# A selection step queued behind the last one-hot compare in a two-layer decoder step with product-key experts

## The chip, the cores and the metric

One core of one Trainium2 chip runs the whole program. The metric is the time of one execution on the device, in microseconds (us). The engines are TensorE (PE; PEld is its weight load), VectorE (DVE), ScalarE (ACT), GpSimd (POOL) and SyncE (SP), which issues most loads. An engine works through its own queue in order.

## What is computed

Two layers of a decoder trunk on 512 prompt tokens and 64 sample tokens, model width 1024, all in fp32. Each layer has token mixers (windowed attention, gated linear attention, pooling) and then a PEER channel mixer, which is where the change lies:

```python
def block(xi):                                   # 128 tokens
    q = jnp.einsum('td,dhk->thk', xi, w_query).reshape(128, 8, 2, 128)
    s = jnp.einsum('thpk,hpnk->thpn', q, sub_keys)
    sv, si = lax.top_k(s, 16)                    # top 16 of 128 keys, both halves
    cand = sv[:, :, 0, :, None] + sv[:, :, 1, None, :]
    cidx = si[:, :, 0, :, None] * 128 + si[:, :, 1, None, :]
    cscore, ci = lax.top_k(cand.reshape(128, 8, 256), 16)
    eidx = jnp.take_along_axis(cidx.reshape(128, 8, 256), ci, axis=-1)
    g = jax.nn.softmax(cscore, axis=-1)
    u = jnp.take(u_tab, eidx, axis=0)
    h = jax.nn.gelu(jnp.einsum('thkd,td->thk', u, xi), approximate=False)
    v = jnp.take(v_tab, eidx, axis=0)
    return jnp.einsum('thk,thkd->td', g * h, v)
```

So each token selects, for each of 8 heads, 16 of 16384 single-neuron experts, and sums their gated outputs.

## The kernel before

The tokens are split. For tokens 0 to 383 the channel mixer is computed densely: the 16384 experts are 128 blocks of 128, every block is computed for all 384 tokens (`expert_h`, then the matmuls into `y`), and the gates, zero where an expert was not selected, are laid out as a dense table in DRAM (`gd`). For tokens 384 to 511 and the 64 sample tokens the selected rows are gathered by indirect DMA (class `Gather`) beside the dense loop. Matmuls of the dense part are made from fp32 split into two parts of fp32r (`hi`, `lo`; three products); the first 12 experts use whole fp32 weights.

Python code traces the instructions; a planner then gives every engine its order, from what is ready in its own model of the machine and from a rank, which is the place in the trace. `tc.high_priority(n)` moves the rank ahead by n instructions (a negative n, back). `tc.issue_after(ins)` makes what is traced in its block on the engine of `ins` come behind `ins` in that engine's queue; it adds no wait for the end of `ins`.

Per layer, in the order of the trace around the change (function `tile_hybrid_step`):

- Line 1174, `_query`: scores and top 16 of the tokens 256 to 511, two tiles of 128 tokens. `sv` and `siu` hold the values and indices; they, the whole copy `x1W` of the tokens, and all work tiles of the selections lie in the pool `sel` (`sp`, line 1163).
- Line 1188, `_slots`: selection (`_select`, some 150 VectorE instructions and one Exp on ScalarE) of tokens 256 to 383 and its transposition on TensorE into `sT2`.
- Line 1190: the matmuls and Gelu of the first LA = 12 experts (`expert_h`) on `x1W`. `h` has LA + 2 = 14 buffers, its PSUM tile `ps_h` two.
- Lines 1191 to 1194, `_spread`: 32 one-hot steps of 4 tokens, in the pool `spread`. Each compares token keys with an iota on VectorE (lines 951, 953, 960), scales by the gate (953's part on ScalarE, line 958), multiplies one-hots on TensorE (line 964) and copies the result into `gst` (ScalarE, line 965). After 8 steps `gst`, one buffer, is stored to `gd` by four DMAs of ScalarE's queue (line 971). `oh` has two buffers, `ps_yr` six. Rank 250 ahead (SPREAD).
- Lines 1195 to 1197, `gat.choose`: selection of tokens 384 to 511 (`_select`, then lines 996 and 997), which gives the row numbers `gidx` and the gates `gB` of the gather. Rank 50 back (LAGS). It issues no DMA here (line 1000 is for the sample tokens).
- Line 1198 closes the pool `sel`. Line 1208 opens the pool `dense` in the room that the two closed pools leave; its tiles are `vr`, `vh`, `vl`, `wh`, `wl`, `gt`.
- Lines 1210 to 1239: the dense loop over 128 experts. `n.tick()` puts the gathers of the samples, then of tokens 384 to 511, between the experts.

Of the kernel before, what the change touches and what calls it, by code (L numbers as in the profile page):

```python
# [16 lines left out]
OP = mybir.AluOpType  # L17
# [27 lines left out]
LAGS = -50  # L45
# [895 lines left out]
def _spread(n, gp, t, sT, new_ps, gt0=None):  # L941

    nc, c = n.nc, n.c
    iota = lambda w: c["iota"][:, None, None, :].to_broadcast([128, w, 4, 128])
    for g in range(128 // GT):
        st = gp.tile([128, 128, GT], F32, name="gst", bufs=n.gst)
        for t4 in range(0, GT, 4):
            tt = g * GT + t4
            oh = gp.tile([128, 2, 4, 128], F32, name="oh", bufs=n.job)
            w = n.act_mul  # L950
            nc.vector.tensor_tensor(oh[:, 1], iota(1)[:, 0], sT[:, 1, tt:tt + 4, None].to_broadcast([128, 4, 128]), op=OP.is_equal)  # L951
            if w:
                nc.vector.tensor_tensor(oh[:, 0, 0:w], iota(1)[:, 0, 0:w], sT[:, 0, tt:tt + w, None].to_broadcast([128, w, 128]),  # L953
                                        op=OP.is_equal)
            for k in range(4):
                gate = sT[:, 2, tt + k:tt + k + 1]
                if k < w:
                    nc.scalar.activation(oh[:, 0, k, :], oh[:, 0, k, :], AF.Copy, scale=gate)
                else:
                    nc.vector.tensor_scalar(oh[:, 0, k, :], c["iota"], sT[:, 0, tt + k:tt + k + 1], gate,  # L960
                                            op0=OP.is_equal, op1=OP.mult)
            ps = new_ps().rearrange("p (a b) -> p a b", a=4)
            for k in range(4):
                nc.tensor.matmul(ps[:, k, :], oh[:, 1, k, :], oh[:, 0, k, :], start=True, stop=True)  # L964
            nc.scalar.copy(st[:, :, t4:t4 + 4], ps.rearrange("p t i -> p i t"))
            if t4 + 4 < GT:
                yield
        if gt0 is not None:
            nc.scalar.copy(gt0[:, t * (128 // GT) + g], st[:, 0:4, :])
        for i in range(4):  # L970
            nc.scalar.dma_start(n.gd[t * (128 // GT) + g, :, i * 32:(i + 1) * 32, :], st[:, i * 32:(i + 1) * 32, :])
        yield
# [72 lines left out]
def tile_hybrid_step(ctx, tc, I, O, L):  # L1045
    nc = tc.nc
    n = Net(ctx, tc, I, O, L)
# [57 lines left out]
    for l in range(L):  # L1105
# [18 lines left out]
        sT = [sa.tile([128, 3, 128], F32, name=f"selT{t}") for t in range(2)]  # L1124

        def first():
            yield from gat.choose(n, l, sa, sv, siu, 2, 1)
            gs = gat.slots(1)
            for t in range(2):
                for k, _ in enumerate(itertools.chain(_slots(n, sa, sv, siu, t, sT[t], n.hring),  # L1130
                                                      _spread(n, sa, t, sT[t], n.hring))):
                    if k % 2 == 0 and n.early:
                        n.early -= 1
                        next(gs)
                    yield
            n.gs = gs
# [28 lines left out]
        for q in range(2):  # L1165
            nc.gpsimd.tensor_tensor(x1W[q][:, :, 0:HB], x1A[0][q][:, :, 0:HB].bitcast(F32), x1A[1][q][:, :, 0:HB].bitcast(F32),
                                    op=OP.add)
# [23 lines left out]
        with tc.tile_pool(name=f"spread{l}", bufs=1) as gp:  # L1191
            with tc.high_priority(SPREAD):
                for _ in _spread(n, gp, 2, sT2, new_y, gt0):
                    pass
        with tc.high_priority(LAGS):
            for _ in gat.choose(n, l, sp, sv, siu, 1, 0):
                pass
        sc.close()
# [231 lines left out]
```

## Time and profile before

| | us |
|---|---|
| median of 3 runs | 4738.8 (4728.3 to 4741.7) |
| the profiled execution, its own time | 4737.0 |
| its span in the trace | 4735.2 |
| TensorE busy | 4530.7 (96% of the span) |
| VectorE busy | 3793.4 (80%) |
| ScalarE busy | 1820.2 (38%) |
| GpSimd busy | 1370.1 (29%) |

Busy time is an average over stages with different limits, so a change in one stage is read from that stage: from the busy time in a stretch of the span, and from the timeline of each engine there. In a timeline a row is a start, a duration, engine, line, operation, output<-input, count, and in brackets how long the engine had been idle before it and what ended that. Rows of several instructions are merged. The two layers show the same stages, at 1237 to 1369 and at 3592 to 3724 us for the part around the change.

### The profile page before, as it was taken

How to read it: one execution, taken by the hardware profiler on the slowest of the kernel's cores; microseconds unless marked ns; L12 is line 12 of the kernel's file. 1: busy time of each engine (PE TensorE's matmuls, PEld its weight loads, DVE VectorE, ACT ScalarE, POOL GpSimd, SP SyncE). 2: the span in 40 equal slices, each digit the busy share in tenths (PEclk: the TensorE clock that was granted, in tenths of full speed). 3: DMA queues.
4: the chain of work that ended last, by engine and by line, in shares of the span. 5: the costliest groups of instructions: out<-in, count | busy, mean ns of one | idle time of the engine just before them, and what ended most of it. 6: DMA issues, size and time to landing. Idle time of an engine off the chain costs nothing. (4 is left out here: it accounts for less than half of the span.)

```text
span 4735.2 us, 69451 instructions
## 1 busy us (share of the span) xinstructions
PE 4530.7 (96%) x25588; PEld 4001.3 (85%) x25588; DVE 3793.4 (80%) x7435; ACT 1820.2 (38%) x3386; POOL 1370.1 (29%) x884
## 2 busy tenths in 40 slices
PE   7999999989999999999999999999999999999998
PEld 6879977788778999999878789777887789999997
DVE  5455698697879999999964556977978799999998
ACT  3434323354343433333344343234433433333333
POOL 0011001121035555555300110011210365555552
PEclk9999999999999999999999999999999999999999
DMA  4334535566379899999723345265663798898996
GB/s 147 110 125 139 180 94 213 193 232 229 126 274 345 328 337 325 330 324 331 279 85 121 122 149 167 88 222 195 232 231 131 289 353 323 328 330 322 335 323 233
DMA packets 359521, 1093.59 MB, mean 231 GB/s; under 512 B 28495, under 2 KB 164175, under 8 KB 309709
## 3 DMA queue, kind: packets, MB, share of 16 engines
q1 hardware_dynamic: 272112, 608.88, 38.0%
q0 software_dynamic: 55296, 402.68, 22.6%
q10 hardware_dynamic: 31772, 77.60, 4.4%
q8 instruction: 201, 3.29, 0.3%
q14 instruction: 140, 1.14, 0.1%
HBM read 1014.01 MB, written 77.52 MB: 231 GB/s over the span
## 5 line engine op out<-in xcount | busy, mean ns | idle before, releaser
L128 POOL TENSOR_TENSOR wlo<-raw,whi 128x1024 fp32r<-128x1024 f32 x232 | 704.1, 3035 | 928.4 <-ACT whi L131 894.1
L131 ACT CAST whi<-raw 128x1024 fp32r<-128x1024 f32 x582 | 607.9, 1048 | 601.0 <-PE ps_mm L183 379.0
L183 PE MATMUL ps_h<-x1A,whi 128*128 128x384 f32 x3712 | 696.4, 340 | 13.3 <-ACT h L1182 13.2
L183 PEld LDWEIGHTS ps_h<-x1A,whi 128*128 128x128 f32 x3712 | 655.9, 190 | 33.6 <-ACT h L1182 17.1
L128 DVE TENSOR_TENSOR wlo<-raw,whi 128x1024 fp32r<-128x1024 f32 x350 | 432.8, 1241 | 275.2 <-ACT whi L131 136.8
L1024 DVE SCALAR_TENSOR_TENSOR zB<-uvr,hc,zB 128x1024 f32<-128x1024 f32 x380 | 587.2, 1545 | 4.7
L1006 POOL DMA_INDIRECT uvr<-uv,gidx x384 | 441.8, 1151 | 474.9 <-DVE zB L1024 209.0
L1017 DVE SCALAR_TENSOR_TENSOR uvr<-uvr,x1B 128x1024 f32<-128x1024 f32 x384 | 493.4, 1285 | 68.9 <-DMA uvr<-uv,gidx 68.6
L1236 PE MATMUL y<-vh,wh 128*128 128x512 f32 x1536 | 478.1, 393 | 0.6 <-ACT vh L131 0.6
L1236 PE MATMUL y<-vl,wh 128*128 128x512 f32 x1536 | 476.5, 391 | 0.0
L1236 PE MATMUL y<-vh,wl 128*128 128x512 f32 x1536 | 474.9, 390 | 0.3 <-DVE wl L128 0.3
L183 PE MATMUL ps_mm<-xa,whi 128*128 128x320 f32 x2400 | 413.3, 321 | 14.7 <-ACT xa L131 14.7
L1225 DVE TENSOR_TENSOR h<-h,gt 128x384 f32<-128x384 f32 x256 | 395.8, 1551 | 11.5 <-ACT h L1182 7.0
L183 PEld LDWEIGHTS ps_mm<-xa,whi 128*128 128x128 f32 x2400 | 370.7, 194 | 33.8 <-ACT xa L131 15.3
L183 PE MATMUL ps_h<-x1A,wlo 128*128 128x384 f32 x1856 | 362.7, 338 | 0.0
L1236 PEld LDWEIGHTS y<-vl,wh 128*128 128x128 f32 x1536 | 288.7, 188 | 64.2 <-DVE vl L128 0.2
L1236 PEld LDWEIGHTS y<-vh,wl 128*128 128x128 f32 x1536 | 288.7, 188 | 63.5 <-DVE wl L128 0.7
L131 ACT CAST wh<-h 128x384 fp32r<-128x384 f32 x256 | 130.5, 511 | 533.3 <-PE y L1236 502.0
L183 PEld LDWEIGHTS ps_h<-x1A,wlo 128*128 128x128 f32 x1856 | 327.1, 189 | 0.0
L1236 PEld LDWEIGHTS y<-vh,wh 128*128 128x128 f32 x1536 | 287.3, 189 | 45.7 <-ACT vh L131 1.4
L1019 ACT ACTIVATE hc<-hc 128x1 f32<-128x1 f32 x384 | 77.7, 203 | 628.1 <-DVE uvr L1017 620.3
L128 DVE TENSOR_TENSOR vl<-vr,vh 128x1024 fp32r<-128x1024 f32 x256 | 311.5, 1217 | 0.7 <-ACT vh L131 0.7
(349 smaller groups left out, 7650.3 us busy)
## 6 DMA issues: line engine op xcount, KB each, us to landing
raw<-wall SPq DMA_DIRECT2D x468, 512.0 KB
raw<-ut SPq DMA_DIRECT2D x256, 512.0 KB
vr<-vt SPq DMA_DIRECT2D x256, 512.0 KB
gd<-gst ACTq DMA_DIRECT2D x96, 512.0 KB
gt<-gd SPq DMA_DIRECT2D x62, 768.0 KB
S<-state_gla SPq DMA_DIRECT2D x8, 1024.0 KB
s_gla<-S ACTq DMA_DIRECT2D x8, 1024.0 KB
uvr<-uv,gidx POOLq DMA_INDIRECT x384
```

What stands on the lines that cost most here:

```text
L128: return eng.tensor_tensor(lo, src, hi.bitcast(F32), op=OP.subtract)
L131: return self.nc.scalar.copy(hi, src), self.sub_lo(lo, src, hi, eng)
L183: self.nc.tensor.matmul(ps[:, 0:W], w[wi][:, k * 128:(k + 1) * 128], xs[xi][k], start=(a == 0 and k == 0), stop=(a == len(pa) - 1 and k == ...
L1006: self.n.nc.gpsimd.indirect_dma_start(out=r, out_offset=None, in_=self.n.I["uv"], in_offset=bass.IndirectOffsetOnAxis(ap=self.idx[t][:, s: ...
L1017: nc.vector.scalar_tensor_tensor(r[:, 0:1024], r[:, 0:1024], 1.0, self.x[t], op0=OP.mult, op1=OP.mult, accum_out=hc[:, 0:1])
L1019: nc.scalar.activation(hc[:, 1:2], hc[:, 0:1], AF.Gelu)
L1024: nc.vector.scalar_tensor_tensor(acc, r[:, 1024:2048], hc[:, 1:2], acc, op0=OP.mult, op1=OP.add)
L1225: nc.vector.tensor_tensor(h3, h3, gt[:, :, i % 4, :], op=OP.mult)
L1236: nc.tensor.matmul(y[t][d], wt[:, ts], vt[:, d * 512:(d + 1) * 512], start=(j == 0 and a == 0), stop=(j == NE - 1 and a == 2))
```

## The change

The last compare of line 951 that was traced is kept in `n.spread`, and the instructions that `gat.choose` traces on VectorE for tokens 384 to 511 are queued behind it. At that place the last one traced is the compare of the 32nd step of `_spread` for tokens 256 to 383.

```diff
@@ _spread
-            nc.vector.tensor_tensor(oh[:, 1], iota(1)[:, 0], sT[:, 1, tt:tt + 4, None].to_broadcast([128, 4, 128]), op=OP.is_equal)
+            n.spread = nc.vector.tensor_tensor(oh[:, 1], iota(1)[:, 0], sT[:, 1, tt:tt + 4, None].to_broadcast([128, 4, 128]), op=OP.is_equal)
@@ tile_hybrid_step
-        with tc.high_priority(LAGS):
+        with tc.high_priority(LAGS), tc.issue_after(n.spread.ins):
             for _ in gat.choose(n, l, sp, sv, siu, 1, 0):
                 pass
```

## Rows read from the trace of the kernel before

**Rows 1.** The page: busy us (share of the span) and instructions of each engine.

```profile
PE 4530.7 (96%) x25588; PEld 4001.3 (85%) x25588; DVE 3793.4 (80%) x7435; ACT 1820.2 (38%) x3386; POOL 1370.1 (29%) x884
```

**Rows 2.** Windows: length, busy PE, PEld, DVE, ACT, POOL, PE clock, DMA share, GB/s.

```profile
1236.90:1263.40 26.50, 24.29 (x72) 14.02 (x73) 25.83 (x159) 5.32 (x8) 0.00 (x0) 0.94 0.20 63
1263.40:1325.50 62.10, 61.31 (x301) 43.38 (x300) 49.36 (x150) 35.65 (x82) 4.71 (x3) 1.00 0.43 151
1325.50:1365.70 40.20, 29.93 (x179) 28.76 (x177) 25.57 (x42) 19.05 (x43) 13.92 (x6) 0.88 0.54 200
1380.00:2360.00 980.00, 977.30 (x4911) 884.73 (x4910) 920.47 (x1057) 378.13 (x642) 519.16 (x272) 1.00 0.90 328
```

**Rows 3.** Timeline of TensorE around the start of the dense stage, first layer.

```profile
1359.31 1.79 PE L183 MATMUL ps_h<-x1A,wlo 128*128 128x384 f32 x8
1365.74 2.93 PE L183 MATMUL ps_h<-x1A,whi 128*128 128x384 f32 x8 [4.65 <-ACT h L1182]
```

**Rows 4.** Timelines of ScalarE and SyncE there; the last row is the second layer's.

```profile
1356.72 2.89 ACTq L971 DMA_DIRECT2D gd<-gst  x4
...
1363.97 0.92 ACT L131 CAST wh<-h 128x384 fp32r<-128x384 f32 x2 [2.93 <-DMA gd<-gst]
...
1364.08 0.80 SPq L1219 DMA_DIRECT2D vr<-vt  x2
...
3718.97 0.81 SPq L1219 DMA_DIRECT2D vr<-vt  x2
```

**Rows 5.** Timeline of VectorE: selection's first and last, last compares; last row second layer.

```profile
1247.32 0.28 DVE L887 TENSOR_TENSOR cand<-sv 128x128 f32<-128x128 f32 x1
...
1306.86 0.29 DVE L997 TENSOR_TENSOR gidx<-key 128x128 int32<-128x128 f32 x1
...
1354.20 0.59 DVE L960 TENSOR_SCALAR oh<-ct,selT 128x128 f32<-128x128 f32 x2
1357.05 1.97 DVE L1225 TENSOR_TENSOR h<-h,gt 128x384 f32<-128x384 f32 x4 [2.25 <-ACT gt L969]
...
3709.84 0.59 DVE L960 TENSOR_SCALAR oh<-ct,selT 128x128 f32<-128x128 f32 x2
```

**Rows 6.** Windows, VectorE alone (DVE busy first); the last row: one-hot tiles, every engine.

```profile
1263.40:1308.70 45.30, 43.26 (x134) 1.00 0.45 161
1239.06:1308.70 69.64, 66.93 (x278) 0.98 0.37 128
...
1239.06:1308.70 69.64, 20.04 (x146) 18.99 (x147) 28.75 (x76) 12.86 (x38) 0.98 0.37 128
```

**Rows 7.** Windows of the one-hot tiles: busy PE, PEld, DVE, ACT, with counts.

```profile
1263.40:1325.50 62.10, 24.59 (x176) 23.50 (x176) 34.86 (x92) 15.63 (x46) 1.00 0.43 151
```

**Rows 8.** Timeline of VectorE: the compare of line 906 in both selections, and what followed.

```profile
1248.21 1.22 DVE L906 TENSOR_TENSOR rstep<-ci,rank 128x2048 bf16<-128x2048 bf16 x1
1249.34 0.19 DVE L887 TENSOR_TENSOR cand<-sv 128x40 f32<-128x40 f32 x1
...
1283.39 1.23 DVE L906 TENSOR_TENSOR rstep<-ci,rank 128x2048 bf16<-128x2048 bf16 x1
1284.65 1.22 DVE L861 TENSOR_TENSOR rprod<-rstep,di 128x2048 bf16<-128x2048 bf16 x1
```

**Rows 9.** Timelines of VectorE and POOL: one-hot compares without and beside POOL's split.

```profile
1347.18 0.42 DVE L953 TENSOR_TENSOR oh<-ct,selT 128x256 f32<-128x256 f32 x1
...
1351.70 2.58 DVE L953 TENSOR_TENSOR oh<-ct,selT 128x256 f32<-128x256 f32 x1
...
1351.48 2.52 POOL L128 TENSOR_TENSOR wlo<-raw,whi 128x1024 fp32r<-128x1024 f32 x1 [8.57 <-PE ps_h L183]
1361.23 2.34 POOL L128 TENSOR_TENSOR wlo<-raw,whi 128x1024 fp32r<-128x1024 f32 x1 [7.23 <-ACT whi L131]
```

**Rows 10.** Windows, TensorE alone: length, busy, granted clock, DMA share, GB/s.

```profile
1365.70:1368.40 2.70, 2.66 (x8) 0.50 0.99 378
...
3723.30:3728.70 5.40, 5.31 (x13) 0.50 1.02 335
```

## The prediction

> **What bounds the kernel now.** I read the page's busy shares first, then busy time by stretch, then the timelines of TensorE, ScalarE, SyncE and VectorE around the change, in both layers. TensorE is busy 96% of the span [rows 1]. The change lies in the turn from the query stage to the dense expert stage. Once the dense stage runs, TensorE has no gaps (977.3 of 980 us) and VectorE is busy 920.5 of 980 [rows 2]: its rate is TensorE's, and only its start can move. So the question is when TensorE's first dense matmul goes.
>
> Ahead of it stand, on TensorE, 12 experts on whole fp32 weights (`x1W`, line 1190), 32 one-hot steps of line 964 and four experts on split weights; 16 is the limit, since `h` has 14 buffers and `ps_h` two. In the first layer that work runs from 1236.9 to 1361.1 [rows 2, 3]; then TensorE idles 4.65 us until a Gelu frees `ps_h` [rows 3]. What it waits for is the hand-over of memory: the last `gst` leaves for DRAM from 1356.72 on, and when it has gone the first `wh` cast (ScalarE, 1363.97) and the first `vr` load (SyncE, 1364.08) start within 0.11 us of each other [rows 4]. Two different tiles, on two engines, neither touched by that transfer, go at one moment: the pool `dense` gets the room of the closed pools as a whole. The second layer repeats it at 3718.97 [rows 4]. The closed pools are two: `spread` (line 1191) and `sel` (closed on line 1198), and `sel` holds every work tile of the moved selection. Today the selection is out of the way: its VectorE work begins at 1247.32 and ends at 1307.15, 47 us before the last compares (1354.2 to 1354.7) [rows 5]. `gst` is the last holder.
>
> **The change, part by part.** It adds no instruction and no byte. It forbids VectorE to issue any instruction of `choose(..., 1, 0)` before the compare of line 951 of the last one-hot step. Its Exp on ScalarE follows by data. No DMA is issued in this selection (line 1000 is for the samples only), so SyncE's and POOL's queues are passed by nothing, and its results `gidx` and `gB` are needed only after the sample gathers that are left, much later.
>
> *What it removes.* The selection leaves the one-hot stage. VectorE was full there: 43.3 of 45.3 us busy between 1263.4 and 1308.7 [rows 6]. But TensorE was fuller, 61.3 of 62.1 us from 1263.4 to 1325.5 [rows 2], and its order is set by the planner. The one-hot steps lead by 250 traced instructions (SPREAD); the 12 experts stand before them with about 10 each (8 matmuls, load, Gelu), 120. A step has 4 VectorE, 3 ScalarE and 4 TensorE instructions, 11, and eight steps 5 more for the store. So the lead is used up, and all 12 experts are ahead, when 250 of these are issued: 250 / 93 x 8 = 21.5 steps. The trace shows just that: up to 1325.5, where the last whole-weight expert ends, 176 one-hot matmul records of 8 a step, 22 steps [rows 7]. The remaining 10 steps and one reload of the single `gst` follow, a tail in which no selection work lies today. TensorE's sum up to 1325.5 doesn't change, so the tail starts at 1325.5 less the idle time of TensorE that the selection causes before: 0.8 us inside the 62.1 [rows 2] plus a few tenths for the first transpose, whose key is interleaved with selection pieces. I take 1.0 us, from 0 to 3. The last compare then ends at 1353.7 instead of 1354.7; in the second layer at 3709.4 (3709.84 + 0.59 - 1.0) [rows 5].
>
> *What it adds.* Behind that compare comes the whole selection, alone. Its price: VectorE was busy 66.93 us from 1239.06 to 1308.70, 28.75 of it on one-hot tiles [rows 6], which leaves 38.2 us for two selections and a scrap of the query: 19.1 each while interleaved. Alone, a dependent instruction starts later: from the 2048-element compare of line 906 to its successor 1.26 us (1283.39 to 1284.65), against 1.13 us where something else follows (1248.21 to 1249.34) [rows 8]. Some 20 links of 0.12 us are 2.4 us more at most; I take half of that and a little, 20.5 us, from 19.1 to 21.5. The Trainium skill, page "VectorE: DVE Perf Modes", section on the TRN2 errata, says that SBUF latency is exposed between instructions; it speaks against a block of dependent instructions. By it the sum below would be 2 us more (21.5 in each layer), by the interleaved price alone 2.8 us less; the 0.13 us of the rows lie with the rule.
>
> Queued behind the selection on VectorE are the dense stage's `h * gt` of line 1225 (four, 1.97 us today at 1357.05, [rows 5]); some may go in between, 0 to 2 us, I take 1. Then the hand-over: first layer 1353.7 + 20.5 + 1.0 = 1375.2 against 1364.0, 11.2 us later; second 3709.4 + 20.5 + 1.0 = 3730.9 against 3719.0, 11.9 later. TensorE cannot hide it: its 16 experts are done at 1361.1 [rows 3]. Every dense expert comes after, so the sum of both, 23.1 us, is added to the end.
>
> *POOL.* Its split of `wlo` works beside the last compares: a `[128,256]` compare beside it took 2.58 us, against 0.42 us elsewhere, and POOL has another split of 2.34 us at 1361.23 [rows 9], which would now fall into the selection: 0 to 2.2 us a layer, taken at 0 in the sum because most of the selection's forms were never seen beside POOL, and kept in the range. The Trainium skill, page "Advanced Engine Details and Errata", section "VectorE Performance Modes", says that VectorE's second SBUF port is shared with GpSimd; by it the sum would be 4.4 us more in both layers, and the row of the stretched compare agrees.
>
> *The clock.* After the idle 4 to 5 us TensorE was granted 0.50, the lower level of 1.2 GHz, from 1365.7 to 1368.4 in the first layer and from 3723.3 to 3728.7 in the second [rows 10]. At half speed 2.7 us lose 1.4 and 5.4 lose 2.7. An idle time of some 15 us should leave both layers like the second or slightly worse: 0 to 5 us in all, I take 2.
>
> Sum: 23.1 + 2 = 25 us on the profiled execution's own 4737.0 us, so 4762; that execution is 1.8 us below the median of the three runs shown, so 4764 is the forecast. Own range: low, in each layer 2 us more gained early, 1.4 less for the selection and 1 less for `h * gt`, and nothing for the clock: 25 - 2 x 4.4 - 2 = 14, 4753; high, in each 1 us less gained early, 1 more for the selection, 1 for `h * gt`, 2.2 for POOL, and 3 more for the clock: 25 + 2 x 5.2 + 3 = 38, 4777.
>
> **The rivals.** *Faster: the freed VectorE lets the one-hot steps run ahead.* A step costs VectorE some 1.5 us; if the steps follow each other at that pace and the experts fill in behind, the last compare may end so early that the selection is over before TensorE has done its 16 experts. It decides at a last compare some 11 us earlier than today, near 1343.5: then nothing is lost. Beyond it the gain is TensorE's idle: 40.2 - 29.9 = 10.3 us from 1325.5 to 1365.7 [rows 2], of which perhaps 9 in each layer can go: 4738.8 - 18 = 4721. Against it speaks the 61.3 of 62.1 and the 22 steps [rows 2, 7]; for it, that the planner's order is made afresh and VectorE was as full as TensorE. Chance 0.13.
>
> *No change: the dense stage doesn't wait for the selection.* If memory is handed over tile by tile and the first tiles lie clear of the selection's, or if the steps end just about 11 us earlier, TensorE restarts near 1365.7 as before; the 20.5 us on VectorE are then made up within the dense stage, where it has 59.5 us to spare in 980 [rows 2]. 4734 to 4746. Against it: `wh` and `vr` starting together [rows 4]. Chance 0.18.
>
> That the change does nothing can be left out: the selection ends 47 us ahead of the last compare today, so the new order must differ.
>
> **How the numbers follow.** Own case 0.69, of which 0.05 lies under the bound of 0.3% (14.2 us, about what a measurement of this kernel can tell from no change); rivals 0.13 and 0.18. So slower 0.64, within 0.3% 0.05 + 0.18 = 0.23, faster 0.13. The own range, 4753 to 4777, holds about 0.6; taking in the case of no change down to 4734, and some spread of runs at the top, the range is 4734 to 4780 and leaves out the faster case and a little more.
>
> **What would show it.** Right, if in the changed kernel's timeline the last instruction of the selection (line 997) ends near 1374 and 3730, the first `vr` load and `wh` cast follow it within a microsecond, not the landing of `gst`, and TensorE idles about 15 us before. The step "the tail doesn't move" is wrong if 26 or more one-hot steps are done when the last whole-weight expert ends, or the last compare ends before 1350. The price of the selection is wrong if it takes less than 19 or more than 23 us alone. The hand-over is wrong if `vr` loads start while the selection runs. The forecast falls altogether if the dense stage starts before 1364.

## The result and the profile after

The changed kernel takes 4780.0 us, median of 4 runs (4769.8 to 4789.9), against 4737.8 us for the kernel before in the same comparison: 1.0088 times as long, 95% interval 1.0073 to 1.0102, or 42 us more (35 to 48). The forecast was 4764, range 4734 to 4780: slower, as said, but by 42 us and not 25. The median lies on the range's upper end.

The profiled execution is the fastest of the four: 4769.8 us, span 4768.0, 32.8 us over the span of before. The other three were granted a mean TensorE clock of 0.973 to 0.976 against its 0.977. So some 10 us of the 42 are in no trace, and the accounts below explain 33. (A clock lower by 0.002 over 4770 us would be some 10 us; that is an estimate.)

The page, then windows of the whole core (columns as in [rows 2]) and, in the last row, of the one-hot tiles alone (columns as in [rows 7]):

```profile
PE 4527.0 (95%) x25588; PEld 3996.9 (84%) x25588; DVE 3792.4 (80%) x7435; ACT 1821.4 (38%) x3386; POOL 1375.0 (29%) x884
...
1263.30:1326.40 63.10, 62.18 (x303) 44.01 (x302) 35.43 (x92) 32.25 (x79) 4.16 (x3) 1.00 0.43 150
1326.40:1382.30 55.90, 31.12 (x179) 29.09 (x177) 48.53 (x145) 22.87 (x47) 14.41 (x6) 0.77 0.44 163
1400.00:2380.00 980.00, 974.46 (x4892) 882.56 (x4892) 910.89 (x1048) 378.61 (x640) 521.53 (x271) 1.00 0.90 325
...
1263.30:1326.40 63.10, 25.79 (x176) 24.38 (x176) 35.43 (x92) 15.84 (x46) 1.00 0.43 150
```

Every engine has as many instructions as before, and the busy times differ by at most 4.9 us (POOL). VectorE is freed up to 1326.4 (35.43 us busy where it was 49.36) and pays from there (48.53 of 55.90 us, against 25.57 of 40.20, [rows 2]), while TensorE has the same 179 matmul records in a stretch 15.7 us longer.

VectorE and, below the dots, POOL around the last one-hot step, first layer; the last row is the second layer's:

```profile
1351.75 0.69 DVE L951 TENSOR_TENSOR oh<-ct,selT 128x512 f32<-128x512 f32 x1 [0.65 <-PE ps_yr L964]
1352.36 2.56 DVE L877 CAST si<-siu 128x256 bf16<-128x256 uint32 x1
...
1356.01 0.42 DVE L953 TENSOR_TENSOR oh<-ct,selT 128x256 f32<-128x256 f32 x1
1362.32 1.90 DVE L960 TENSOR_SCALAR oh<-ct,selT 128x128 f32<-128x128 f32 x1
1364.27 0.32 DVE L960 TENSOR_SCALAR oh<-ct,selT 128x128 f32<-128x128 f32 x1
1367.58 1.02 DVE L1225 TENSOR_TENSOR h<-h,gt 128x384 f32<-128x384 f32 x2
1378.80 0.29 DVE L997 TENSOR_TENSOR gidx<-key 128x128 int32<-128x128 f32 x1
...
1352.13 2.56 POOL L128 TENSOR_TENSOR wlo<-raw,whi 128x1024 fp32r<-128x1024 f32 x1 [6.30 <-PE ps_h L183]
1361.79 2.34 POOL L128 TENSOR_TENSOR wlo<-raw,whi 128x1024 fp32r<-128x1024 f32 x1 [7.11 <-ACT whi L131]
...
3747.50 0.29 DVE L997 TENSOR_TENSOR gidx<-key 128x128 int32<-128x128 f32 x1
```

The selection begins with the cast of line 877, right behind the compare of line 951 and in the middle of the 32nd step, whose own compares (953, 960) now stand among the selection's instructions.

ScalarE, SyncE and TensorE at the hand-over, and the second layer's `vr` load and TensorE row:

```profile
1366.16 3.08 ACTq L971 DMA_DIRECT2D gd<-gst  x4
1379.17 1.34 ACT L131 CAST wh<-h 128x384 fp32r<-128x384 f32 x3 [12.72 <-DVE gidx L997]
1380.53 1.28 ACT L1182 ACT_TABLE_LOAD   x1
1381.82 0.49 ACT L1182 ACTIVATE h<-ps_h 128x384 f32<-128x384 f32 x1
...
1379.23 1.28 SPq L1219 DMA_DIRECT2D vr<-vt  x3
3747.93 1.28 SPq L1219 DMA_DIRECT2D vr<-vt  x3
...
1364.27 1.22 PE L964 MATMUL ps_yr<-oh 128*128 128x128 f32 x4 [2.62 <-DVE oh L960]
1382.36 1.65 PE L183 MATMUL ps_h<-x1A,whi 128*128 128x384 f32 x4 [16.87 <-ACT h L1182]
1383.81 1.61 PE L1236 MATMUL y<-vh,wh 128*128 128x512 f32 x3
...
3751.06 1.65 PE L183 MATMUL ps_h<-x1A,whi 128*128 128x384 f32 x4 [16.87 <-ACT h L1182]
```

`gidx` is written until 1379.09; 0.08 us later ScalarE casts `wh` and 0.14 us later SyncE loads `vr`. Neither reads `gidx`. Before, both waited for the `gst` store [rows 4]; now the store is over by 1373, since from there to 1379 the DMA engines move nothing. TensorE idles 16.87 us in both layers, against 4.65 us in the first layer of before [rows 3] and 4.03 in its second.

For the comparisons below, from the timelines: a layer's stage starts with the first matmul on `x1W`. The columns give, in us and for the first / second layer, the first `vr` load and the first `y` matmul after that start, and the length of the dense stage (first to last `y`).

| kernel | median | first `vr` | first `y` | dense stage |
|---|---|---|---|---|
| before | 4737.8 | 127.2 / 126.9 | 131.6 / 131.3 | 997.5 / 998.5 |
| changed | 4780.0 | 140.3 / 141.7 | 144.9 / 146.3 | 1003.8 / 1002.2 |
| e2_whole_step | 4777.6 | 142.8 / 142.5 | 147.4 / 147.1 | 999.5 / 1004.1 |
| e3_layer0 | 4756.4 | 140.5 / 125.7 | 145.1 / 130.1 | 1004.9 / 999.7 |
| e4_before_twice | 4750.8 | 132.6 / 132.6 | 137.0 / 137.2 | 1000.1 / 998.5 |
| e5_step16 | 4749.1 | 129.5 / 129.8 | 134.0 / 134.4 | 998.2 / 1000.0 |
| e5_step24 | 4761.1 | 135.9 / 136.2 | 140.4 / 140.8 | 1000.0 / 1000.2 |
| e1_room_before | 4752.8 | 128.9 / 128.0 | 136.7 / 135.6 | 996.7 / 999.8 |
| e1_own_room | 4775.6 | 133.7 / 134.8 | 139.6 / 140.9 | 1006.9 / 1007.8 |
| e6_room_low | 4788.2 | 128.0 / 126.6 | 134.4 / 134.3 | 1017.7 / 1020.1 |
| e7_clean_before | 4750.5 | 128.1 / 127.3 | 135.7 / 134.9 | 999.9 / 999.1 |
| e7_clean_room | 4773.5 | 141.8 / 143.5 | 146.3 / 148.1 | 1002.7 / 1001.1 |
| e8_before_la14 | 4758.5 | 137.3 / 137.7 | 141.8 / 142.2 | 996.6 / 998.4 |
| e8_after_la14 | 4792.5 | 150.4 / 148.4 | 154.9 / 153.0 | 998.9 / 1001.8 |

Of the 32.8 us of span: the first `y` is 13.3 and 15.0 later, the dense stages are 6.3 and 3.7 longer (38.3 in all); the first layer's stage began 2.1 later, and the stretch from the first layer's last `y` to the second layer's stage was 7.5 shorter (1226.1 to 1218.6). The last two I can't attribute: nothing of the change lies there, but the planner lays those stretches anew.

### The profile page after: what moved, and what is told of

It reads as the page before. It is cut to its first block, busy times and chain, and to the rows that moved or that the text cites. A ratio compares the mean times of both kernels' runs of the same rounds, so it can differ in the third digit from the quotient of the medians.

```text
span 4768.0 us, 69449 instructions
## 1 busy us (share of the span) xinstructions
PE 4527.0 (95%) x25588; PEld 3996.9 (84%) x25588; DVE 3792.4 (80%) x7435; ACT 1821.4 (38%) x3386; POOL 1375.0 (29%) x884
## 5 line engine op out<-in xcount | busy, mean ns | idle before, releaser
L1024 DVE SCALAR_TENSOR_TENSOR zB<-uvr,hc,zB 128x1024 f32<-128x1024 f32 x380 | 565.8, 1489 | 4.7
L183 PE MATMUL ps_mm<-xa,whi 128*128 128x320 f32 x2400 | 412.6, 321 | 13.4 <-ACT xa L131 13.3
```

What stands on the lines that cost most here:

```text
L183: self.nc.tensor.matmul(ps[:, 0:W], w[wi][:, k * 128:(k + 1) * 128], xs[xi][k], start=(a == 0 and k == 0), stop=(a == len(pa) - 1 and k == ...
L1024: nc.vector.scalar_tensor_tensor(acc, r[:, 1024:2048], hc[:, 1:2], acc, op0=OP.mult, op1=OP.add)
```

## Experiments

An edit that adds lines shifts the line numbers behind it: 999 and 1007 below are line 997 of before, 1221, 1234 and 1235 are line 1219, 1240 is line 1225 and 1251 is line 1236.

**Is it the late last step, or the end of the selection?** The changed kernel lets selection instructions in between the compares of the 32nd step, whose matmuls so wait until 1364.27. This run queues the selection behind the whole step:

```diff
-            n.spread = nc.vector.tensor_tensor(oh[:, 1], ...)
+            nc.vector.tensor_tensor(oh[:, 1], ...)
...
-                    nc.vector.tensor_scalar(oh[:, 0, k, :], ...)
+                    n.spread = nc.vector.tensor_scalar(oh[:, 0, k, :], ...)
```

> The changed kernel with the selection queued behind the last gated one-hot (L960) instead of the last compare (L951), so that the last one-hot step is whole and its matmuls are not late. Hand-over theory: L960 ends near 1354 us and the last gst copy near 1356, but L997 still ends near 1376 to 1379 and the first vr load and wh cast start with it; time 4772 to 4784, that of the changed kernel within 8 us. Rival, the delayed last one-hot step carries the loss: 4738 to 4750.

Measured 4777.6 us (1.0090 times before, 1.0073 to 1.0107), the changed kernel's time. VectorE, POOL and SyncE:

```profile
1355.87 0.59 DVE L960 TENSOR_SCALAR oh<-ct,selT 128x128 f32<-128x128 f32 x2
1356.38 0.37 DVE L877 CAST si<-siu 128x256 bf16<-128x256 uint32 x1
...
1367.82 3.30 DVE L861 TENSOR_TENSOR rprod<-rstep,di 128x2048 bf16<-128x2048 bf16 x1
1380.76 0.29 DVE L997 TENSOR_TENSOR gidx<-key 128x128 int32<-128x128 f32 x1
...
1367.71 2.34 POOL L128 TENSOR_TENSOR wlo<-raw,whi 128x1024 fp32r<-128x1024 f32 x1 [12.04 <-ACT whi L131]
...
1381.11 1.28 SPq L1219 DMA_DIRECT2D vr<-vt  x3
```

The last step is whole and 8 us earlier (1356.5 against 1364.6), and nothing is won: `vr` goes 0.06 us after `gidx`. The late step is not the cause. This run also gives the selection's price by itself: 24.67 us from 1356.38 to 1381.05, less four `h * gt` of some 0.5 us each, less 2.1 us by which one product ran beside POOL (3.30 us, elsewhere 1.22): 20.6 us.

**Each layer for itself.**

```diff
-        with tc.high_priority(LAGS), tc.issue_after(n.spread.ins):
+        with tc.high_priority(LAGS), ExitStack() as qc:
+            if l == 0:
+                qc.enter_context(tc.issue_after(n.spread.ins))
```

> The changed kernel with the wait in layer 0 alone; layer 1's selection is placed as in the kernel before. Hand-over theory: each layer loses its own 13 to 15 us at the first y and a few more behind it: 4753 to 4762, 4758 as one number. Rival, the loss grows only in the last layer's end (where the last gathers and the dense experts finish together): 4738 to 4744. Rival, layer 0's delay is absorbed by layer 1: 4770 to 4780 falls to 4738.

Measured 4756.4 us (1.0041, 1.0019 to 1.0062): 19 us (9 to 29), some half of 42. In the table the first layer looks like the changed kernel, the second like before. The losses are two of a kind, and the first layer's loss is not made up in the second.

**From which place does it cost?** The selection queued behind the 16th or the 24th compare instead of the 32nd:

```diff
+            if tt // 4 < 16:                     # 24 in the other run
+                n.spread = sp_                   # sp_: this step's compare
```

> The changed kernel with the selection queued behind the 16th compare of the spread (it started at 1294.71 us in layer 0 of the changed kernel's profile) instead of the 32nd (1351.75). Hand-over theory: the selection runs in VectorE's idle time while TensorE paces steps 17 to 26, L997 ends near 1325 to 1345, before the last one-hot step, and nothing is lost: 4733 to 4746. Rival, any place behind the first steps costs the selection's own time: 4755 to 4780.

> The changed kernel with the selection queued behind the 24th compare (1326.78 us in layer 0 of the changed kernel's profile). Hand-over theory: from there VectorE has 22.2 us of steps (1325.50 to 1354.50 of the kernel before) and 20.5 us of selection, so the later of the two ends near 1369, 5 us behind the hand-over of the kernel before: 4744 to 4760, 4751 as one number, with L997 between 1355 and 1372. Rival, no break-even in this stretch, all or nothing: 4733 to 4742 or 4772 to 4784.

Measured 4749.1 us (1.0026, 1.0015 to 1.0037) and 4761.1 us (1.0056, 1.0039 to 1.0073): 12 and 24 us over before, each a little above the range given. VectorE's `gidx` and SyncE's `vr` behind the 24th compare:

```profile
1370.64 0.29 DVE L999 TENSOR_TENSOR gidx<-key 128x128 int32<-128x128 f32 x1
...
1371.18 1.28 SPq L1221 DMA_DIRECT2D vr<-vt  x3
```

And behind the 16th, `gidx` and ScalarE's first `wh`:

```profile
1322.30 2.23 DVE L999 TENSOR_TENSOR gidx<-key 128x128 int32<-128x128 f32 x1
...
1359.71 1.34 ACT L131 CAST wh<-h 128x384 fp32r<-128x384 f32 x3 [2.85 <-DMA gd<-gst]
```

Behind the 24th the selection is still the last holder; it shares VectorE with eight steps, and the last step is 8 us later than in before. Behind the 16th the selection is over 35 us before the hand-over, which the `gst` store sets again; what is left is a last step 2 to 3 us later in each layer. The profiled run, the second fastest of ten, shows 3.6 of the 12 us. So the place from which the selection is the last holder lies between the two, and a place behind the first steps that costs nothing was not found. 12, 24, 42 us for 16, 24, 32 is a slope and not a step, as if the selection cost what of it finds no idle VectorE time before the hand-over; these runs fit that, they don't isolate it.

**How much idle VectorE time is there?** The kernel before with the selection done twice in its old place:

```diff
-            for _ in gat.choose(n, l, sp, sv, siu, 1, 0):
-                pass
+            for _ in range(2):
+                for _ in gat.choose(n, l, sp, sv, siu, 1, 0):
+                    pass
```

> The kernel before (no wait) with the selection of tokens 384 to 511 done twice, the second over the first's tiles with the same outcome: 20.5 us more of VectorE work in each layer, at the place where the kernel before has it. Slack theory: in the kernel before VectorE is idle for 10.7 us in 1308.70 to 1325.50 and for 6.8 us in 1325.50 to 1354.50, so 10 to 17 of the 20.5 us hide and the hand-over moves by 0 to 10 us a layer: 4738 to 4758, 4746 as one number. Rival, VectorE is owed the whole selection wherever it stands: 41 us more, 4775 to 4783.

Measured 4750.8 us (1.0027, 1.0007 to 1.0048). The second selection ends at 1348.5 us, the last step 5.6 us later than in before, and so does the hand-over (5.5 / 5.6 us in the table). So of the second selection's 20.5 us about 15 hide. That is the kind of room the change gives up: behind the last compare none of it hides.

**Does the dense stage wait for the selection's memory?** Its work tiles, and those of `_slots`, get a room of their own on the other side of the memory (pool `own`); only `gt`, first needed by expert 4, is put there later. To make the space, buffers of `s2` and `cv` are reduced and `rsum` lies in `cand`.

```diff
+        kc, kp = scope(f"own{l}", side="right")
...
-            for _ in gat.choose(n, l, sp, sv, siu, 1, 0):
+            for _ in gat.choose(n, l, kp, sv, siu, 1, 0):
...
-                    gt = dp.tile([128, TD // GT, 4, GT], F32, name="gt", bufs=2)
+                    gt = gp2.tile([128, TD // GT, 4, GT], F32, name="gt", bufs=2)
```

> The changed kernel, but the selection's tiles lie in a room of their own on the other side of the memory, and only the gt tiles (first needed by expert 4) are put there afterwards; vr, vh, vl, wh and wl wait only for the x1W and one-hot memory. Everything else is as in the changed kernel. Hand-over theory: the first vr load and wh cast start at the end of the last one-hot step (near 1366 us of layer 0, not near 1379), L997 still ends near 1379, PE's wait for the first y falls from 16.9 us to 3 to 7 us, and 20 to 30 of the 42 us come back: 4738 to 4758, 4748 as one number. Rival, the delayed last one-hot step carries the loss: 4770 to 4785. Rival, VectorE's late work falls due in the dense stage wherever the memory lies: the first y comes early, but the time stays at 4765 to 4785.

> The kernel before with the same change of rooms (no wait on the last compare): the control for e1_own_room. Hand-over theory and both rivals: within 8 us of the kernel before, 4730 to 4746, since the selection ends near 1307 us, some 57 us ahead of the hand-over. What this kernel is off by is taken from e1_own_room.

Measured 4775.6 us (1.0085, 1.0068 to 1.0102), and 4752.8 us (1.0035, 1.0022 to 1.0047) for the control: 23 us between them, not 10. Both miss what the theory gave, and 4775.6 lies in the ranges of both rivals (of which e2_whole_step speaks against the first). SyncE, VectorE and TensorE of e1_own_room:

```profile
1364.08 22.90 SPq L1234 DMA_DIRECT2D vr<-vt  x7
1387.03 5.66 SPq L1230 DMA_DIRECT2D gt<-gd  x2
...
1386.50 0.29 DVE L1007 TENSOR_TENSOR gidx<-key 128x128 int32<-128x128 f32 x1
...
1400.70 1.22 PE L1251 MATMUL y<-vh,wh 128*128 128x512 f32 x2 [5.85 <-ACT wh L131]
```

TensorE alone behind that wait (length, busy, granted clock):

```profile
1400.70:1406.40 5.70, 5.70 (x14) 0.51 1.02 408
```

One half is shown: `vr` now starts 22 us before the selection ends, so it was the memory that held it. The other half is the edit's own fault: the first `gt` load had inherited the wait. It goes 0.24 us after `gidx`, lands 12.5 us later beside the other loads, and TensorE waits 5.85 us for expert 4 (5.77 in the second layer). Behind the wait it has 5.7 us of work at the lower clock, which costs some 2.8 us more. Together that is 8.7 of the 10.2 us by which the first dense stage is longer than the control's; in the second it is 8.6, and the stage is 8.0 longer. So the trace leaves next to nothing for the second rival, work that VectorE owes. What else it shows is a first `y` that is 2.9 and 5.3 us later than the control's (the profiled execution is 14 us below the median, so this is no account of the whole 23 us). The control, too, is 15 us over before, with a first `y` 4 to 5 us later; that its `wl` splits came later on VectorE is what its ScalarE waited for, but why the planner put them so I did not trace.

**The same with the selection ranked far lower**, so that VectorE does the first dense work ahead of it:

```diff
-        with tc.high_priority(LAGS), tc.issue_after(n.spread.ins):
+        with tc.high_priority(-3000), tc.issue_after(n.spread.ins):
```

> e1_own_room with the selection planned at a much lower rank (-3000 in place of -50), so that VectorE does the dense stage's first splits and products ahead of what is left of it. If what e1_own_room still loses against its control (23 us) is the order on VectorE around the hand-over (last one-hot step split, wl and vl splits behind the selection): 4752 to 4763. If VectorE is owed those 20 us a layer in the dense stage in any order: 4768 to 4780, no better than e1_own_room.

Measured 4788.2 us (1.0107, 1.0090 to 1.0124), no better than the changed kernel and above both ranges given. The hand-over is back where it was (first `y` at 134.4 / 134.3, even earlier than in the control e1_room_before), and all of the loss against that control is in the dense stage, 20 us a layer. VectorE, SyncE and TensorE there:

```profile
1417.94 0.29 DVE L1007 TENSOR_TENSOR gidx<-key 128x128 int32<-128x128 f32 x1
1423.68 1.50 DVE L1240 TENSOR_TENSOR h<-h,gt 128x384 f32<-128x384 f32 x3 [5.45 <-DMA gt<-gd]
...
1418.26 1.08 SPq L1230 DMA_DIRECT2D gt<-gd  x2
...
1424.84 1.22 PE L1251 MATMUL y<-vh,wh 128*128 128x512 f32 x2 [10.04 <-ACT wh L131]
```

The numbers are nearest to "VectorE is owed 20 us in any order", but the rows give another reason for the larger part: `gt` was held until 1418.23, and TensorE stood 10.04 us for it, 13.91 in the second layer. With the lower clock behind these waits (granted 0.61 from 1424.8 to 1431.5, 0.68 from 3808.1 to 3815.0) that is some 12.6 of 21 and 16.1 of 20 us. What the remainder is the run does not decide.

**The wait moved off `gt` too.** Half of the `gt` tiles go back among the dense tiles, and only the one of expert 8 into the room; the rank table goes into `zB`.

```diff
-                    gt = gp2.tile(...)
+                    gt = (dp, gp2)[i // 4 % 2 == 0].tile([128, TD // GT, 4, GT], F32, name="gt", bufs=1)
```

> The control for e7_clean_room: the kernel before, with the selection's tiles in a room of their own, one gt tile of the two (that of experts 4 to 7, 12 to 15 and so on) among the dense tiles and only the other (first needed by expert 8) in the selection's room, the rank table kept in zB and the gates made in place. All theories: 4740 to 4760, near the 4753 of e1_room_before.

> The changed kernel in the rooms of e7_clean_before. In e1_own_room and e6_room_low the wait had only moved: the first gt load stood behind the selection's end (it was issued at 1387.0 and 1418.3 us and landed some 12 to 17 us later), and TensorE waited 5.8 and 10.0 us for expert 4. Hand-over theory: without that wait no row of TensorE waits on a gt load, the first y is 3 to 5 us a layer behind the control's (as in e1_own_room), the dense stage 0 to 4 us longer, in all 6 to 18 us over e7_clean_before, 13 as one number. Rival, VectorE is owed the selection's 20 us a layer right behind the hand-over, where it has no slack: 22 to 40 us over e7_clean_before, as e1_own_room (23) or more.

Measured 4750.5 us (1.0032, 1.0021 to 1.0043) and 4773.5 us (1.0086, 1.0054 to 1.0118), 23 us apart, a number in the rival's range. VectorE and SyncE of the second:

```profile
1374.01 0.29 DVE L1007 TENSOR_TENSOR gidx<-key 128x128 int32<-128x128 f32 x1
...
1374.44 1.28 SPq L1235 DMA_DIRECT2D vr<-vt  x3
```

The room was not apart. The dense tiles take 51 kB of a partition, and beside the room 50.94 kB are left: 64 bytes of them reach into it. Three `vr` tiles are 12 kB, and yet all three go from 0.14 us after `gidx` on, the three first `wh` casts with them. So the run says nothing of VectorE's debt, and it says of the hand-over what none of the others does so well: the pool waits as a whole, for any overlap. The changed kernel itself bears this out: in its plan of the memory the three `vr` tiles lie exactly where `x1W` lay, in no tile of the selection, and they wait for it all the same. In e1_own_room the plan leaves a gap between the dense tiles and the room, and there `vr` did not wait. A room that is separate for all `gt` tiles too was not run.

**More work for TensorE in the wait.** 14 instead of 12 experts ahead, in the changed kernel and in before. To make the space, the selection's work tiles are in a pool opened behind the query; that pool has no control of its own.

```diff
-LA = 12
+LA = 14
...
+        wc, tp = scope(f"selw{l}")
```

> The changed kernel with 14 instead of 12 experts begun ahead of the dense stage (two more h buffers; the selection's work tiles in a pool opened behind the query, to make the room). TensorE has 7.8 us more to do before the first y of each layer, and 7.8 us less behind it. Theory, the loss is TensorE's idle time at the hand-over for want of work: part of its 16.9 us is filled, 4 to 8 us a layer come back: 4764 to 4772. Rival, TensorE sets the pace of the one-hot steps, so that the last compare and all behind it move by as much: 4775 to 4785.

> The kernel before with the same 14 experts ahead. Theory: its waits of 4.7 us at the hand-over and 2.4 us behind it are filled in part, 2 to 6 us a layer: 4725 to 4733, which would be faster than both kernels. Rival, TensorE paces the one-hot steps and everything moves by as much: 4734 to 4742.

Measured 4792.5 us (1.0121, 1.0093 to 1.0149) and 4758.5 us (1.0044, 1.0028 to 1.0061), both beyond even the rival. The second is slower than before; the first is slower than the changed kernel by its median, with intervals that overlap. Against before, the first `y` of e8_before_la14 is 10 us later in both layers, and the dense stage, with two experts' `expert_h` less, is at most 0.9 us shorter. A window of it in e8_before_la14 (columns as in [rows 2]) and TensorE's waits in it, in us in total, times, longest:

```profile
1378.80:2375.80 997.00, 988.76 (x4938) 891.32 (x4938) 924.82 (x1076) 378.30 (x644) 519.96 (x272) 1.00 0.90 326
...
PE y L1240 <- DVE vl L128: 4.1, 3, 2.8
PE ps_h L183 <- ACT h L1185: 4.0, 3, 2.7
```

TensorE has 6.4 us less to do there than in before (988.76 against 995.20 in 997.9 us) and waits 8.2 us instead of 2.7. None of the kernels that were run is faster than the one before.

## Why the prediction was right, and where it was short

The profiled run (4769.8) lies in the own range, 4753 to 4777, and the median above it. In part this is luck: 10 us in the dense stages that were not foreseen stand against a stretch that is 7.5 us shorter for reasons not known.

*The tail doesn't move: right.* 176 one-hot records, 22 steps, up to the end of the last whole-weight expert, as in [rows 7], although VectorE had 14 us less to do there. The last compare of line 951 stands 112.8 us after the stage's start in the first layer (before 114.2) and 114.2 in the second (114.6): 1.4 and 0.4 us earlier, taken at 1.0. (The row of the first layer's last compare makes 1353.8, where the sum has 1353.7; and the sign for the second layer, 3730, left out that the first layer's delay moves it: line 997 ended at 3747.8, 141.6 us after its stage's start.)

*The selection's price: right.* 20.6 us (e2_whole_step, by subtraction) against 20.5.

*The hand-over: right in mechanism, short in size.* Predicted 11.2 and 11.9 us later, 23.1; measured 13.1 and 14.8, 27.9. Two terms carry most of the difference. POOL was taken at 0: its splits lie beside the selection twice, and the cast of line 877 took 2.56 us instead of 0.37, the `tensor_scalar` of line 960 1.90 instead of 0.32. The first only replaces the stretched compare of before [rows 9]; the second, 1.6 us, is new. And `h * gt` was taken at 1 us: all four go between, some 2 us. Together some 2.5 us; from the start of the last compare of line 951 to the end of `gidx` it was 27.3 us where the terms of the sum make 25.2 (3.7 for the step in before, 20.5, 1.0), 2.1 more in each layer. Both terms were in the range, at its upper end. The Trainium skill, page "SBUF — State Buffer", section "A bandwidth-pool intuition that's wrong (but worth ruling out)", calls this a lock, not a sharing of bandwidth. The rows agree: the two stretched instructions here and the product of e2_whole_step end at 1354.92, 1364.22 and 1371.12 us, where POOL's end plus their own time alone is 1355.06, 1364.45 and 1371.27.

*The clock: 2 us predicted, nothing measured.* TensorE alone at the restart, two windows of before, then two of the changed kernel (length, busy, granted clock):

```profile
1368.40:1370.10 1.70, 1.70 (x5) 0.51 0.98 343
...
3721.80:3723.30 1.50, 1.00 (x4) 0.51 1.01 374
...
1382.30:1387.60 5.30, 5.24 (x13) 0.50 1.05 335
...
3751.00:3756.50 5.50, 5.44 (x13) 0.50 1.03 316
```

The prediction misread its own rows: the window of [rows 10] ends at 1368.4, but the lower level went on to 1370.1, and in the second layer it began at 3721.8. With both windows TensorE worked 4.36 and 6.31 us at the lower level before, 10.67 in all, and 5.24 and 5.44 in the changed kernel, 10.68. So either way 5.3 us are lost, and 16.87 us without work cost no more clock than 4 to 5 did.

*The dense stage is not only its start: this step failed.* The prediction held that only the start can move, since TensorE has no gaps after it, and its sum has nothing for the rest. But the dense stages are 6.3 and 3.7 us longer. TensorE stands still in them for 5.5 and 6.4 us, where it was 2.7 and 2.2: that is 7.0 of the 10.0 us. The lower clock inside them costs 7.3 us in place of 6.8, and 2.5 are left over. With the selection behind the 24th or 32nd compare the seven dense stages of the kernels without a room took 999.5 to 1004.9 us, against 997.5 to 1000.1 in the seven where it stands earlier (before, e3_layer0's second layer, e4_before_twice, e5_step16); the two behind the 24th, 1000.0 and 1000.2, do not stand out. TensorE's waits in the first stage, of before and of the changed kernel:

```profile
PE ps_h L183 <- ACT h L1182: 2.4, 2, 2.0
...
PE ps_h L183 <- ACT h L1182: 5.5, 3, 2.5
```

They all fall in the first 100 us. Behind two of the changed kernel's waits, of 2.46 and 2.12 us, the granted clock falls to 0.50 for 3.4 us each; before it did so once, behind 2.03 us. In the second layer it does so once before, behind 1.86 us, and not at all in the changed kernel, whose longest wait there is 1.83 us. ScalarE at the longest of the changed kernel's waits:

```profile
1444.80 0.20 ACT L1019 ACTIVATE hc<-hc 128x1 f32<-128x1 f32 x1 [5.15 <-DVE uvr L1017]
1444.91 0.47 ACT L1182 ACTIVATE h<-ps_h 128x384 f32<-128x384 f32 x1
```

The Gelu that TensorE waits for stands behind a small one of the gather (line 1019), which waited 5.15 us for VectorE. e8_before_la14 tells the same from the other side: with 6.4 us less TensorE work the stage shortened by 0.9 and 0.1. That VectorE, busy 93% of that stage, sets its pace there together with TensorE fits all of this; no run isolates it.

*Slower and not faster.* The rival that the freed VectorE lets the steps run ahead fell with the 22 steps; its break-even was put at a last compare 11 us earlier, and it came 1.4 and 0.4 us earlier. That the dense stage might not wait fell with `vr` 0.14 us behind `gidx`, and e1_own_room and e7_clean_room show that the memory is what it waits for. What stays open: the 10 us by which the median exceeds the profiled run, what the 2.5 us left over in the dense stages are, and whether a room that is apart for every tile would give back what the hand-over costs; no kernel with the late selection was run that does.

## What to carry to other kernels

Work taken off a busy engine's queue is worth nothing where another engine sets the pace, and where it is put it may find no idle time to hide in: before moving a block, look for the idle time of its engine in the old place (here about 15 of the 20.5 us of a second selection hid there) and in the new. A pool that is opened in another's room may wait for the last user of that room, even for a tile it hardly touches; so the scratch tiles of a step that can be late should not lie where the next stage's first tiles will be. And when a wait is removed by moving memory, look at once which tile has inherited it.

## What was not expected of the hardware

- *A table load on the path.* The selection's Exp and the dense stage's Gelu need different tables on ScalarE. Before, both loads (1.28 us) lay among the one-hot steps, at 1283.48 and 1292.04; with the selection last, the load for Gelu stands at 1380.53, behind the hand-over and ahead of the Gelu for which TensorE waits. From the first `wh` to that Gelu it takes 2.65 us instead of 1.24 (before: 1363.97 to 1365.21). Little of it reaches the first `y`, which comes 4.6 us after the first `vr` instead of 4.4, since four matmuls on `ps_h` stand ahead of it and not eight. The Trainium skill, page "ScalarE: Activation LUTs", section "What ACT_TABLE_LOAD costs", gives 1283 ns for the load, which the row bears out. The 1380 ns of drain that it adds for a switch do not show: the load starts 0.02 us behind the last `wh` cast.
- *A load asked for in the busy start lands late.* In e1_own_room, with a DMA share of 1.00 from 1387.0 to 1404.7, two `gt` loads of 768 KB took 12.5 and 17.2 us to land; over that run's 62 they took 7.7 to 17.2, median 11.4. A hand-over that delays only this one tile still cost TensorE 5.85 us there and 10.04 us in e6_room_low.
